# Up projection of a ConvFFN: block sums finished in PSUM under the convolution, four raw weight tiles, the next pair's weights prepared between the products, row sums partly on PE

## The chip, the cores and the metric

The kernel runs on one core of one Trainium2 chip. The metric is device time in microseconds (us) of one execution of the whole program. Engines are named as in the profile: PE is TensorE (matmul), DVE is VectorE, ACT is ScalarE, POOL is GpSimd, SP is SyncE, which here only issues DMAs.

## What is computed

One layer of an encoder trunk over 1024 tokens of width 1024: a hybrid mixer, a memory cross-attention and a gated MLP with a convolution of width three. The change touches the last of these alone:

```
gu = rms_norm(x, ffn_norm) @ w_up
gu = depthwise_conv(gu, ffn_conv_w, ffn_conv_b, FFN_CONV // 2, FFN_CONV // 2)
g, u = gu[..., :D_FF], gu[..., D_FF:]
x = x + (jax.nn.silu(g) * u) @ w_down
```

D_FF is 2816, so w_up has 5632 columns, and the up projection gives 22 blocks of 128 columns of g and the 22 blocks of u that belong to them. A block of g with its block of u is called a pair here.

## The kernel before

**Numbers.** Every matmul works in two parts: an operand is split into a rounded part and the remainder (ACT copies to the rounded type, DVE or POOL subtracts), and three matmuls per product (rounded by rounded, rounded by remainder, remainder by rounded) add up in PSUM. The normalised input h lies in SBUF transposed and split (`h3`), as 2 halves of 512 tokens.

**Up projection, plain pairs.** The first two pairs (`up_plain`, PLAIN is 2) are ordinary products: for g and u each, 24 matmuls of 128x512 for each of the two token halves, into a PSUM bank, which ACT copies (L1221) into an SBUF row.

**Up projection, fast pairs.** The other 20 pairs (`up_fast`) compute the 2x2 block product (rows of w_up in two halves, tokens in two halves) with seven block products instead of eight. `combos(k)` prepares, once for the stage, the needed sums T1 to T4 of the blocks of h: for each of four k, DVE (L1170 and neighbours) and POOL subtract the rounded parts and the remainders, and `put` splits the result again. For each pair POOL makes four sums S1 to S4 of the weight blocks, and `wop` splits seven weight operands. `prod` is one block product: 12 matmuls of 128x512. Products accumulate in three banks a_, b_ and c_: a_ takes w11 by B11 and then w12 by B21; b_ takes w2 by T2, then w3 by T3, then w22 by T4; c_ takes w1 by T1, then w4 by B22. Between them the block sums are read out: p1 (ACT, L1258) holds a_ after its first product, u2 (DVE, L1260) is b_ plus p1, p5 (ACT) is c_ after its first, u3 (DVE, L1267) is b_ after T3 plus p1. The results go into two SBUF rows `rows_` (a row for g, one for u): L1264 (ACT), L1268, L1270 and L1272 (DVE).

**Convolution and gate.** `gate` then works on the SBUF rows: for g and for u each, one ACT pass for the middle tap and the bias (L1201) and two DVE passes for the outer taps (L1202, L1203); then a tanh on ACT (L1207), two DVE passes (L1208, L1209) and a store of 512 KB to a scratch tensor `actd` in DRAM (L1210).

**Down projection.** For two halves of 512 tokens: 22 steps k, each loads a piece of actd (`ar`, L1297) and a piece of w_down (L1302), splits both, and runs 24 matmuls into eight banks. The residual tiles `xr` (L1292) are loaded at the start of each half.

**What sets the order.** The order in which each engine takes its instructions is fixed when the program is built: a scheduler with a simulated timeline interleaves the written code, so the products of one pair stand between those of the next. Each engine then runs its list strictly in that order, and waits on semaphores of the others. The tile pools track a tile as a whole (reuse_waits="tile"): an instruction that writes any part of a tile waits for the earlier readers of any part. The weight loads and the stores share SP's queue.

Of the kernel before, what the change touches and what calls it, by code (L numbers as in the profile page):

```python
# [83 lines left out]
def trunk_layer(ctx: ExitStack, tc: tile.TileContext, a: dict, out: bass.AP):  # L84
# [1076 lines left out]
    def combos(k):  # L1161

        d, e = tmpf("t3", "S1"), tmpf("e3", "S2")
        dve.tensor_sub(d, f(B22[0])[:, k, :], f(B12[0])[:, k, :])
# [5 lines left out]
        dve.tensor_sub(t1, f(B12[0])[:, k, :], f(B11[0])[:, k, :])  # L1170
# [24 lines left out]
    def gate(i):
        gu = []
        for s_ in range(2):
            jj = s_ * NF + i
# [2 lines left out]
            act.activation(g, r_[:, 1:S + 1], AF.Identity, bias=fcv[:, 3, jj:jj + 1], scale=fcv[:, 1, jj:jj + 1])  # L1201
            dve.scalar_tensor_tensor(g, r_[:, 0:S], fcv[:, 0, jj:jj + 1], g, ALU.mult, ALU.add)  # L1202
            dve.scalar_tensor_tensor(g, r_[:, 2:S + 2], fcv[:, 2, jj:jj + 1], g, ALU.mult, ALU.add)  # L1203
# [8 lines left out]
    def up_plain(i):  # L1212
        for s_ in range(2):
            with tc.issue_after(last_rs[-6 + s_ if i == 0 else -1].ins):
                wh, wl = wunit(up_load(i, s_))
            for c in (1, 0):
                ps = bank()
                for k in range(KD):
                    mm3(ps, wh[:, k * P:(k + 1) * P], wl[:, k * P:(k + 1) * P],
                        h3[c][0][:, k, :], h3[c][1][:, k, :], k == 0, k == KD - 1)  # L1220
                act.activation(rows_[s_][:, 1 + c * 512:513 + c * 512], ps, AF.Copy)  # L1221
# [118 lines left out]
```

## Time and profile before

| what | us |
|---|---|
| median of 3 runs (1516.84 to 1522.0) | 1517.36 |
| the profiled execution's own time | 1518.07 |
| its span | 1516.3 |
| plain pairs, from about | 768 |
| first fast pair, from about | 819 |
| fast pairs from the second, from about | 854 |
| up projection's last matmul, at | 1251.39 |
| down projection's first matmul, at | 1270.63 |

All times within the run are from the start of the span of one profiled execution, which is 0.7 us above the median. A row of the windows view gives, for a stretch of time, each engine's busy time with its count of instructions, then the clock that PE was granted (1.00 is full speed), the busy share of the DMA engines, and GB/s. A row of the timeline gives start, duration, engine, line, operation and tiles, and in square brackets how long the engine had been idle and what released it. PE's records carry a modelled end, so the distance from one start to the next is the better measure of its pace. In the groups by tile a row ends its name with the count, then least, median and largest duration in ns, the first and last start, and the shape.

### The profile page before, as it was taken

Reading aid. Unit: us, or ns where it says so; the run is one execution under the profiler, and the core shown is the slowest. Engines: PE = TensorE matmul, PEld = TensorE weight load, DVE = VectorE, ACT = ScalarE, POOL = GpSimd, SP = SyncE. Lnnn points to the kernel's source line nnn. Section 1 sums busy time; section 2 is a strip of 40 time slices with the busy share of each in tenths; the row PEclk is TensorE's granted clock in tenths of the full one; section 3 lists DMA queues with packets and bytes.
Section 4 is the critical chain, followed back from the end, with each engine's and each line's share of the span. In section 5 each row is a group of like instructions: output and inputs, shape, how many; then the busy total and the mean of one; then the engine's idle time right before and its main releaser. Section 6 shows DMA issues by size and latency. Waiting matters only on the chain.

```text
span 1516.3 us, 18284 instructions
## 1 busy us (share of the span) xinstructions
PE 1372.4 (91%) x6756; PEld 1147.3 (76%) x6756; DVE 1038.4 (68%) x1346; ACT 715.7 (47%) x1194; POOL 731.1 (48%) x688
## 2 busy tenths in 40 slices
PE   6887789898999999999977999999999995999998
PEld 5766678787888888888865777777777774888887
DVE  5889886899998854676688667667666693334332
ACT  5265665688888831455324434434444451222220
POOL 7768685556687610111374887776667600000000
PEclk9989889999999999999998899999999997999999
DMA  5211010200000141102210222122222235446541
GB/s 179 66 33 34 25 43 29 97 1 2 1 1 1 49 160 42 56 2 70 98 42 14 89 77 84 56 83 84 79 61 84 72 134 175 146 144 203 184 144 63
DMA packets 88024, 113.95 MB, mean 75 GB/s; under 512 B 6634, under 2 KB 61183, under 8 KB 87935
## 3 DMA queue, kind: packets, MB, share of 16 engines
q1 hardware_dynamic: 87935, 112.78, 23.0%
q8 instruction: 53, 0.87, 0.2%
q14 instruction: 36, 0.29, 0.1%
HBM read 92.84 MB, written 19.92 MB: 74 GB/s over the span
## 4 chain that ended last, share of the span: by engine, by line
PE 42%; DVE 19%; POOL 9%; DMA 5%; ACT 5%; issue 5%; SPq 0%; DVEq 0%; POOLq 0%; ACTq 0%
PE bank L109 16%; PE psP L109 5%; DMA raw<-in_w_up 5%; PE psq L109 3%; PE psmo L109 3%; PE psS L109 3%; PE po L109 2%; POOL S L1248 2%; DVE wop L1227 2%; DVE st L753 2%; POOL S L1243 2%; POOL S L1244 2%; DVE gu L1202 2%; DVE pT L776 2%; PE psT L772 2%
## 5 line engine op out<-in xcount | busy, mean ns | idle before, releaser
L109 PE MATMUL bank<-whi,ah 128*128 128x512 f32 x352 | 138.4, 393 | 18.8 <-ACT ah L1300 18.8
L109 PE MATMUL bank<-wlo,ah 128*128 128x512 f32 x352 | 138.1, 392 | 0.0
L109 PE MATMUL bank<-whi,al 128*128 128x512 f32 x352 | 135.6, 389 | 0.0
L1301 DVE TENSOR_TENSOR al<-ar,ah 128x512 fp32r<-128x512 f32 x44 | 30.4, 693 | 147.1 <-ACT ah L1300 138.3
L1227 POOL TENSOR_TENSOR wop<-S,wop 128x512 fp32r<-128x512 f32 x80 | 127.0, 1613 | 7.7 <-ACT wop L1226 7.7
L1234 PE MATMUL bank<-h,wop 128*128 128x512 f32 x320 | 125.6, 393 | 5.2 <-ACT p L1258 3.7
L1235 PE MATMUL bank<-h,wop 128*128 128x512 f32 x320 | 125.0, 391 | 0.0
L1236 PE MATMUL bank<-h,wop 128*128 128x512 f32 x320 | 124.5, 390 | 0.0
L1234 PE MATMUL bank<-T,wop 128*128 128x512 f32 x240 | 96.8, 403 | 30.4 <-DVE row L1272 14.5
L1300 ACT ACTIVATE ah<-ar 128x512 fp32r<-128x512 f32 x44 | 27.8, 632 | 177.3 <-PE bank L109 161.8
L109 PE MATMUL psS<-kT,qT 96*128 96x512 f32 x384 | 103.9, 404 | 5.3 <-ACT pr L757 5.2
L759 POOL TENSOR_SCALAR pr<-pr,st 128x1024 f32<-128x1024 f32 x64 | 72.0, 1126 | 53.9 <-DVE st L758 32.1
L1236 PE MATMUL bank<-T,wop 128*128 128x512 f32 x240 | 95.4, 398 | 2.8 <-POOL wop L1227 2.8
L1227 DVE TENSOR_TENSOR wop<-raw,wop 128x512 fp32r<-128x512 f32 x40 | 44.6, 1117 | 74.3 <-ACT wop L1226 58.2
L1235 PE MATMUL bank<-T,wop 128*128 128x512 f32 x240 | 95.2, 397 | 0.0
L1202 DVE SCALAR_TENSOR_TENSOR gu<-row,fcw,gu 128x1024 f32<-128x1024 f32 x44 | 68.6, 1560 | 34.3 <-ACT gu L1201 34.3
L109 PEld LDWEIGHTS bank<-whi,ah 128*128 128x128 f32 x352 | 66.9, 190 | 33.1 <-ACT ah L1300 19.3
L1226 ACT ACTIVATE wop<-S 128x512 fp32r<-128x512 f32 x80 | 47.6, 621 | 91.1 <-POOL S L1244 91.0
L776 DVE TENSOR_TENSOR pT<-psT,pT 128x512 fp32r<-128x512 f32 x128 | 84.5, 679 | 6.2 <-ACT pT L775 6.1
L109 PE MATMUL psin<-hT,whi 128*128 128x512 f32 (+1 forms) x288 | 87.4, 386 | 1.1 <-ACT hT L200 1.0
L757 ACT ACTIVATE pr<-psS,st,rqk 128x1024 f32<-128x1024 f32 x64 | 77.2, 1206 | 18.5 <-DVE st L755 14.0
L753 DVE TENSOR_REDUCE st<-psS 128x1 f32<-128x1024 f32 x64 | 77.7, 1214 | 8.0 <-PE psS L109 8.0
(347 smaller groups left out, 3877.5 us busy)
## 6 DMA issues: line engine op xcount, KB each, us to landing
raw<-in_w_up SPq DMA_DIRECT2D x44, 512.0 KB
raw<-in_w_down SPq DMA_DIRECT2D x44, 512.0 KB
actd<-th SPq DMA_DIRECT2D x22, 512.0 KB
...
```

What stands on the lines that cost most here:

```text
L109: return pe.matmul(ps, lhsT=l, rhs=r, start=start, stop=stop)
L753: dve.tensor_reduce(st[:, 0:1], psS, AX.X, ALU.max, negate=True)
L757: act.activation(pr, psS, AF.Exp, bias=st[:, 1:2], scale=r, accum_out=st[:, 2:3])
L759: scaled[s] = pool.tensor_scalar(pr, pr, st[:, 3:4], 0.0, ALU.mult, ALU.add)
L776: dve.tensor_sub(pTs[s // 2][n][1][:, :, qi * P:(qi + 1) * P], pv, f(dh))
L1202: dve.scalar_tensor_tensor(g, r_[:, 0:S], fcv[:, 0, jj:jj + 1], g, ALU.mult, ALU.add)
L1226: act.activation(o[:, :512], src, AF.Copy)
L1227: (pool if eng == "pool" else dve).tensor_sub(o[:, 512:], src, f(o)[:, :512])
L1234: pe.matmul(ps, lhsT=wh, rhs=bh, start=first and k == 0, stop=False, skip_group_check=True)
L1235: pe.matmul(ps, lhsT=wh, rhs=bl, start=False, stop=False, skip_group_check=True)
L1236: pe.matmul(ps, lhsT=wl, rhs=bh, start=False, stop=k == HK - 1, skip_group_check=True)
L1301: dve.tensor_sub(al, ar, f(ah))
```

## The change

A PSUM tile is now two banks wide (128x1024), and there are four. Each fast pair has two of them: G holds a_ and c_, the two token halves of g; U holds b_ and d_, those of u. The block sums are finished in place: DVE writes d_ = c_ + u3 (L1289), c_ += u2 (L1294) and b_ += p1 (L1298) into PSUM; p5, the SBUF rows and their copies are gone. The convolution (`conv`) reads the PSUM tile: ACT at L1199, DVE at L1200 and L1201 over 1023 columns. `p1` is copied at L1280, u2 made at L1283, u3 at L1288. Raw weights have four tiles, two each for g and u, and are loaded two pairs ahead; `prep` gives the next pair's sums and splits (L1225 on ACT, L1226 on DVE or POOL) as a list of steps, of which `run` puts one or two between the products. In `combos` the first two differences are made by 8 matmuls with plus and minus the identity (`idr`), 32 in all, and the other sums on DVE alone. The operands of the first two steps of the down projection are prepared at the end of the last pair (`first_down`); ah, al and ar take over tiles of the up projection, two of each; the residual tiles are loaded late in a half (the scheduler places them).

```diff
-    pf = psF.enter_context(tc.tile_pool(name="pf", bufs=8, space=PSUM, reuse_waits="tile"))
+    pf = psF.enter_context(tc.tile_pool(name="pf", bufs=4, space=PSUM, reuse_waits="tile"))
...
-    tpl = fs.enter_context(tc.tile_pool(name="tpl", bufs=3, side="right", reuse_waits="tile"))
+    tps = ExitStack()
+    tpl = tps.enter_context(tc.tile_pool(name="tpl", bufs=3, side="right", reuse_waits="tile"))
...
-    def bank():
-        return pf.tile([P, 512], F32, tag="bank", name="bank")
+    def banks():
+        return pf.tile([P, S], F32, tag="bank", name="bank")
...
+        ps = banks()
+        for o, x, y in ((0, B12, B11), (512, B22, B12)):
+            dst = ps[:, o:o + 512]
+            mm(dst, idr[:, 0], x[0][:, k, :], True, False)
+            mm(dst, idr[:, 0], x[1][:, k, :], False, False)
+            mm(dst, idr[:, 1], y[0][:, k, :], False, False)
+            mm(dst, idr[:, 1], y[1][:, k, :], False, True)
+        t1 = tmpf("t1", ("p1", "u2", "u3", "th")[k])
         t1s.append(t1)
...
+        act.activation(t1, ps[:, :512], AF.Copy)
+        put(T3, k, ps[:, 512:])
+        t2 = tmpf("t2", "S1")
+        dve.tensor_sub(t2, f(B22[0])[:, k, :], t1)
         dve.tensor_add(t2, t2, f(B22[1])[:, k, :])
         put(T2, k, t2)
...
+        t4 = tmpf("t4", "S2")
+        dve.tensor_sub(t4, f(B21[0])[:, k, :], t2)
         dve.tensor_add(t4, t4, f(B21[1])[:, k, :])
         put(T4, k, t4)
...
+    idr = fp.tile([P, 2, P], F32R, name="idr")
+    act.activation(idr[:, 0], ident, AF.Copy)
+    act.activation(idr[:, 1], ident, AF.Copy, scale=-1.0)
...
+        raw = (wp.tile([P, S], F32, tag="raw", bufs=2, name="rw") if s_ == 0 else
+               fp.tile([P, S], F32, tag="rw", bufs=2, name="rw"))
+        c0 = s_ * DFF + i * P
+        nc.sync.dma_start(raw.rearrange("p (k c) -> p k c", k=KD),
+                          a["w_up"][0, :, c0:c0 + P].rearrange("(k p) c -> p k c", p=P))
+        return raw
+
+    def conv(i, s_, ps):
+        jj = s_ * NF + i
+        g = fp.tile([P, S], F32, tag=("g", "u")[s_], name="gu")
+        act.activation(g, ps, AF.Identity, bias=fcv[:, 3, jj:jj + 1], scale=fcv[:, 1, jj:jj + 1])
+        dve.scalar_tensor_tensor(g[:, 1:], ps[:, :S - 1], fcv[:, 0, jj:jj + 1], g[:, 1:], ALU.mult, ALU.add)
+        dve.scalar_tensor_tensor(g[:, :S - 1], ps[:, 1:], fcv[:, 2, jj:jj + 1], g[:, :S - 1], ALU.mult, ALU.add)
+        return g
...
+    raws = {}
...
+    def prep(i):
+
+        if i >= NF:
+            return [], {}
+        rg, ru = raws.pop(i)
+        A11, A12, A21, A22 = rg[:, :512], rg[:, 512:], ru[:, :512], ru[:, 512:]
+        w, S_ = {}, {}
+
+        def split(name, src, eng):
+            def go():
+                v = src() if callable(src) else src
+                o = w[name] = wp.tile([P, 1024], F32R, tag="w", name="wop")
+                act.activation(o[:, :512], v, AF.Copy)
+                eng.tensor_sub(o[:, 512:], v, f(o)[:, :512])
+            return go
+
+        def summed(j, op, x, y):
+            def go():
+                S_[j] = tmpf(f"S{j}")
+                op(S_[j], x() if callable(x) else x, y() if callable(y) else y)
+            return go
+
+        steps = [split("11", A11, dve),
+                 summed(1, pool.tensor_add, A21, A22), summed(2, pool.tensor_sub, lambda: S_[1], A11),
+                 split("2", lambda: S_[2], dve), split("1", lambda: S_[1], pool),
+                 summed(3, pool.tensor_sub, A11, A21), split("3", lambda: S_[3], pool),
+                 split("12", A12, dve),
+                 summed(4, pool.tensor_sub, A12, lambda: S_[2]), split("4", lambda: S_[4], pool),
+                 split("22", A22, dve)]
+        return steps, w
...
+    def load_pair(i):
+        if i < NF:
+            raws[i] = (up_load(i, 0), up_load(i, 1))
...
+    def up_plain(i, nxt):
+        raw = raws.pop(i)
+        gu = []
+        for s_ in range(2):
+            wh, wl = wsplit(raw[s_])
+            ps = banks()
+            for c in (1, 0):
+                for k in range(KD):
+                    mm3(ps[:, c * 512:(c + 1) * 512], wh[:, k * P:(k + 1) * P], wl[:, k * P:(k + 1) * P],
+                        h3[c][0][:, k, :], h3[c][1][:, k, :], k == 0, k == KD - 1)
+            gu.append(conv(i, s_, ps))
+            for k in range((2 * i + s_) * HK // (2 * PLAIN), (2 * i + s_ + 1) * HK // (2 * PLAIN)):
+                combos(k)
+        gate(i, *gu)
...
+    def up_fast(i, w, nxt):
+        G, U = banks(), banks()
+        a_, c_, b_, d_ = G[:, :512], G[:, 512:], U[:, :512], U[:, 512:]
+        p1, u2, u3 = tmpf("p1"), tmpf("u2"), tmpf("u3")
+        prod(a_, w["11"], B11, True)
         act.activation(p1, a_, AF.Copy)
-        prod(b_, w2, T2, True)
+        run(nxt, 1)
+        prod(b_, w["2"], T2, True)
         dve.tensor_add(u2, b_, p1)
-        prod(c_, w1, T1, True)
-        act.activation(p5, c_, AF.Copy)
-        prod(a_, w12, B21, False)
-        act.activation(rG[:, lo], a_, AF.Copy)
-        prod(b_, w3, T3, False)
-        u3 = tmpf("u3")
+        run(nxt, 2)
+        prod(c_, w["1"], T1, True)
+        run(nxt, 2)
+        prod(b_, w["3"], T3, False)
         dve.tensor_add(u3, b_, p1)
-        dve.tensor_add(rU[:, hi], u3, p5)
-        prod(c_, w4, B22, False)
-        dve.tensor_add(rG[:, hi], c_, u2)
-        prod(b_, w22, T4, False)
-        dve.tensor_add(rU[:, lo], b_, p1)
-        gate(i)
-
+        dve.tensor_add(d_, c_, u3)
+        run(nxt, 2)
+        prod(a_, w["12"], B21, False)
+        run(nxt, 1)
+        prod(c_, w["4"], B22, False)
+        dve.tensor_add(c_, c_, u2)
+        g = conv(i, 0, G)
+        run(nxt, 2)
+        prod(b_, w["22"], T4, False)
+        dve.tensor_add(b_, b_, p1)
+        u = conv(i, 1, U)
+        run(nxt, len(nxt))
+        if i == NF - 1:
+            first_down.extend([down_in(0, 0), down_in(0, 1)])
+        gate(i, g, u)
+
+    def down_in(s_, k):
+        o = k % 2
+        ar = tmpf("ar", ("S1", "S2")[o])
+        nc.sync.dma_start(ar, actd[k, :, s_ * 512:(s_ + 1) * 512])
+        ah, al = tmpf("ah", ("S3", "S4")[o], F32R), tmpf("al", ("u2", "u3")[o], F32R)
+        act.activation(ah, ar, AF.Copy)
+        dve.tensor_sub(al, ar, f(ah))
+        wh, wl = wunit(lambda raw: nc.sync.dma_start(raw, a["w_down"][0, k * P:(k + 1) * P, :]), eng="ad")
+        return ah, al, wh, wl
...
+    with tc.issue_after(last_rs[-6].ins):
+        load_pair(0)
+    load_pair(1)
     for i in range(PLAIN):
-        up_plain(i)
-        for k in range(i * HK // PLAIN, (i + 1) * HK // PLAIN):
-            combos(k)
+        up_plain(i, None)
+        load_pair(i + 2)
...
+    nxt, w = prep(PLAIN)
+    run(nxt, 4)
...
+    run(nxt, len(nxt))
     for i in range(PLAIN, NF):
-        up_fast(i)
-    fs.close()
+        load_pair(i + 2)
+        nxt, w2 = prep(i + 1)
+        up_fast(i, w, nxt)
+        w = w2
+    tps.close()
 
...
-    dq = dn.enter_context(tc.tile_pool(name="dq", bufs=3, reuse_waits="tile"))
+    dq = dn.enter_context(tc.tile_pool(name="dq", bufs=3, side="right", reuse_waits="tile"))
...
     for s_ in range(2):
+        pss = [banks() for _ in range(4)]
+        ops = [down_in(s_, 0), down_in(s_, 1)] if s_ else first_down
+        for ts in ((0, 1), (2, 3)):
+            for k in range(2):
+                for t in ts:
+                    down_mm(pss[t], t, k, ops[k])
         xr_ = []
-        for t in range(4):
-            xt = dq.tile([P, D], F32, tag="xr", bufs=5, name="xr2")
-            nc.sync.dma_start(xt, x2d[s_ * 4 + t])
-            xr_.append(xt)
...
+        for k in range(2, NF):
+            ops = down_in(s_, k)
...
+            if k >= NF - 5 and len(xr_) < 4:
+                xt = dq.tile([P, D], F32, tag="xr", bufs=6, name="xr2")
+                nc.sync.dma_start(xt, x2d[s_ * 4 + len(xr_)])
+                xr_.append(xt)
```

**A fast pair in the middle.** On PE, of the change: G and U of pair n are bank_8426 and bank_8427, of pair n+1 bank_8567 and bank_8568, of n+2 bank_8708. One row stands for the 12 matmuls of a product (the first one; for w1 by T1 also the third); T1 is h310, B11 is h300.

```order
L1248 MATMUL bank_8427<-T3_7329,wop_8357 128x512 [waits DVE_49]
...
L1248 MATMUL bank_8568<-T2_7328,wop_8476 128x512 [waits DVE_49]
...
L1248 MATMUL bank_8426<-h300_6939,wop_8372 128x512 [waits DVE_49]
...
L1248 MATMUL bank_8426<-h310_7164,wop_8394 128x512
...
L1248 MATMUL bank_8427<-T4_7330,wop_8414 128x512
...
L1248 MATMUL bank_8567<-h310_7164,wop_8479 128x512 [waits Activation_49]
...
L1250 MATMUL bank_8567<-h310_7164,wop_8479 128x512 [waits Pool_49]
...
L1248 MATMUL bank_8708<-h300_6939,wop_8585 128x512 [waits DVE_49,PE_49]
```

And before: pair n has bank_8304 (a_), bank_8305 (b_) and bank_8306 (c_), pair n+1 bank_8449 to bank_8451, pair n+2 bank_8594.

```order
L1234 MATMUL bank_8306<-h310_7164,wop_8298 128x512 [waits Activation_49]
...
L1234 MATMUL bank_8450<-T2_7328,wop_8429 128x512
...
L1234 MATMUL bank_8451<-h310_7164,wop_8432 128x512
L1234 MATMUL bank_8304<-h300_6939,wop_8290 128x512 [waits Activation_49]
...
L1234 MATMUL bank_8305<-T3_7329,wop_8294 128x512 [waits DVE_49]
...
L1234 MATMUL bank_8594<-h300_6939,wop_8569 128x512
...
L1234 MATMUL bank_8305<-T4_7330,wop_8301 128x512 [waits DVE_49]
...
L1234 MATMUL bank_8451<-h310_7164,wop_8443 128x512 [waits Activation_49]
```

Before, the product w1 by T1 of pair n+1 (bank_8451) had a bank of its own and stood ahead of pair n's w12, w3 and w22 products; now it follows pair n's last product (bank_8427 by T4) and writes the same tile bank_8567 that p1 reads, with a wait on ACT.

On ACT, of the change, the same place: gu_8529 and gu_8551 are the convolutions of g and u of pair n, p1_8569 belongs to pair n+1, th_8558 is pair n's tanh.

```order
L1199 ACTIVATE gu_8529<-bank_8426,fcw_309 128x1024 [waits DVE_49]
L1225 ACTIVATE wop_8696<-rw_8424 128x512 [waits DMAHW0_49,PE_49]
L1199 ACTIVATE gu_8551<-bank_8427,fcw_309 128x1024 [waits DVE_49,Activation_49]
L1280 ACTIVATE p1_8569<-bank_8567 128x512 [waits Activation_49]
L1206 ACTIVATE th_8558<-gu_8529 128x1024 [waits DMAHW4_49,DVE_49,Activation_49]
```

On DVE, of the change, the same place:

```order
L1294 TENSOR_TENSOR bank_8426<-bank_8426,u2_8429 128x512 [waits PE_49]
L1200 SCALAR_TENSOR_TENSOR gu_8529<-bank_8426,fcw_309,gu_8529 128x1023 [waits Activation_49]
L1298 TENSOR_TENSOR bank_8427<-bank_8427,p1_8428 128x512 [waits PE_49]
L1226 TENSOR_TENSOR wop_8696<-rw_8424,wop_8696 128x512 [waits DMAHW0_49,Activation_49]
L1201 SCALAR_TENSOR_TENSOR gu_8529<-bank_8426,fcw_309,gu_8529 128x1023 [waits DVE_49]
L1200 SCALAR_TENSOR_TENSOR gu_8551<-bank_8427,fcw_309,gu_8551 128x1023 [waits Activation_49]
L1283 TENSOR_TENSOR u2_8570<-bank_8568,p1_8569 128x512 [waits Activation_49]
```

p1 of pair n+1 stands on ACT behind both convolution passes of pair n, the second of which waits on DVE (L1298); L1298 stands on DVE behind the first convolution pass of DVE (L1200), which waits for ACT's L1199.

**The start of the plain pairs.** On DVE, before: L917 makes the remainders of the last two groups of h, L1170 the first differences of `combos`.

```order
L917 TENSOR_TENSOR h311_7165<-psn_7288,h310_7164 128x4x128 [waits Activation_49]
L1170 TENSOR_TENSOR t1_7473<-h310_7164,h300_6939 128x512 [waits DVE_49,PE_49]
L1170 TENSOR_TENSOR t1_7495<-h310_7164,h300_6939 128x512
L1170 TENSOR_TENSOR t1_7646<-h310_7164,h300_6939 128x512
L1170 TENSOR_TENSOR t1_7668<-h310_7164,h300_6939 128x512
L917 TENSOR_TENSOR h311_7165<-psn_7295,h310_7164 128x4x128 [waits Activation_49]
```

And in the change:

```order
L917 TENSOR_TENSOR h311_7165<-psn_7288,h310_7164 128x4x128 [waits Activation_49]
L917 TENSOR_TENSOR h311_7165<-psn_7295,h310_7164 128x4x128 [waits Activation_49]
L1226 TENSOR_TENSOR wop_7680<-rw_7507,wop_7680 128x512 [waits DMAHW1_49,Activation_49]
L1200 SCALAR_TENSOR_TENSOR gu_7395<-bank_7346,fcw_309,gu_7395 128x1023 [waits Activation_49]
```

The four differences stood between the two L917 and are gone from DVE.

**From up to down.** On SP, before, behind the last pair's store (th_10586):

```order
L1302 DMA raw_10870<-in_w_down 128x1024
L1210 DMA actd_7306<-th_10586 128x1024
L1292 DMA xr2_10596<-x2d_7305 128x1024
...
L1292 DMA xr2_10602<-x2d_7305 128x1024
L1297 DMA ar_10612<-actd_7306 128x512
L1297 DMA ar_10648<-actd_7306 128x512
```

And in the change, first the loads of the first two steps, then what stands behind the store of the pair before the last (th_10387):

```order
L1312 DMA raw_10501<-in_w_down 128x1024
...
L1308 DMA ar_10507<-actd_7306 128x512
L1308 DMA ar_10495<-actd_7306 128x512
...
L1209 DMA actd_7306<-th_10250 128x1024
```

```order
L1209 DMA actd_7306<-th_10387 128x1024
L1312 DMA raw_10694<-in_w_down 128x1024
L1308 DMA ar_10616<-actd_7306 128x512
L1312 DMA raw_10730<-in_w_down 128x1024
L1308 DMA ar_10580<-actd_7306 128x512
L1358 DMA xr2_11156<-x2d_7305 128x1024
...
L1358 DMA xr2_12014<-x2d_7305 128x1024
L1312 DMA raw_10766<-in_w_down 128x1024
```

The first two loads of ar moved ahead of three stores; six residual loads now stand ahead of a w_down load of a later step (raw_10766), and before, four of them stood ahead of the first ar.

More of the change, by code (lines that the diff above doesn't have):

```diff
@@ L1150, in trunk_layer, with tmpf @@
     T2, T3, T4 = tnew("T2"), tnew("T3"), tnew("T4")
-    def tmpf(name, tag=None):
-        return fp.tile([P, 512], F32, tag=tag or name, name=name)
+    def tmpf(name, tag=None, dt=F32):
+        return fp.tile([P, 512], dt, tag=tag or name, name=name)
     def put(dst, k, v):
@@ L1210, in gate @@
         nc.sync.dma_start(actd[i], th)
[L1212 to L1221, printed above, removed]
-        gate(i)
-    def wop(src, eng="pool"):
-        o = wp.tile([P, 1024], F32R, tag="w", name="wop")
-        act.activation(o[:, :512], src, AF.Copy)
-        (pool if eng == "pool" else dve).tensor_sub(o[:, 512:], src, f(o)[:, :512])
-        return o
+    raws = {}
[25 more added lines that the diff above has]
+        return steps, w
     def prod(ps, w, b, first):
@@ L1236, in prod, with run @@
             pe.matmul(ps, lhsT=wl, rhs=bh, start=False, stop=k == HK - 1, skip_group_check=True)
-    def up_fast(i):
-        rg, ru = wload(up_load(i, 0)), wload(up_load(i, 1))
-        A11, A12, A21, A22 = rg[:, :512], rg[:, 512:], ru[:, :512], ru[:, 512:]
-        S1, S2, S3, S4 = [tmpf(f"S{j}") for j in range(1, 5)]
-        w11 = wop(A11)
-        pool.tensor_add(S1, A21, A22)
-        pool.tensor_sub(S2, S1, A11)
-        w2 = wop(S2)
-        w1 = wop(S1)
-        w12 = wop(A12, "dve")
-        pool.tensor_sub(S3, A11, A21)
-        w3 = wop(S3)
-        pool.tensor_sub(S4, A12, S2)
-        w4 = wop(S4)
-        w22 = wop(A22, "dve")
-        rG, rU = rows_
-        lo, hi = slice(1, 513), slice(513, 1025)
-        a_, b_, c_ = bank(), bank(), bank()
-        p1, u2, p5 = tmpf("p1"), tmpf("u2"), tmpf("p5")
-        prod(a_, w11, B11, True)
+    def run(steps, n):
+        for _ in range(min(n, len(steps))):
+            steps.pop(0)()
@@ L1287, in trunk_layer @@
-    dq = dn.enter_context(tc.tile_pool(name="dq", bufs=3, reuse_waits="tile"))
-    for s_ in range(2):
-        xr_ = []
-        for t in range(4):
-            xt = dq.tile([P, D], F32, tag="xr", bufs=5, name="xr2")
-            nc.sync.dma_start(xt, x2d[s_ * 4 + t])
-            xr_.append(xt)
-        pss = [[bank() for _ in range(2)] for _ in range(4)]
-        for k in range(NF):
-            ar = dq.tile([P, 512], F32, tag="ar", name="ar")
-            nc.sync.dma_start(ar, actd[k, :, s_ * 512:(s_ + 1) * 512])
-            ah = dq.tile([P, 512], F32R, tag="ah", name="ah")
-            al = dq.tile([P, 512], F32R, tag="al", name="al")
-            act.activation(ah, ar, AF.Copy)
-            dve.tensor_sub(al, ar, f(ah))
-            wh, wl = wunit(lambda raw: nc.sync.dma_start(raw, a["w_down"][0, k * P:(k + 1) * P, :]), eng="ad")
-            for t in range(4):
-                for half in range(2):
-                    mm3(pss[t][half], ah[:, t * P:(t + 1) * P], al[:, t * P:(t + 1) * P],
-                        wh[:, half * 512:(half + 1) * 512], wl[:, half * 512:(half + 1) * 512], k == 0, k == NF - 1)
+        load_pair(i + 2)
```

45 lines of the change are left out of this document (10 added, 35 removed).

## The prediction

> **What bounds the kernel now.** First the windows, cut at the stages of the feed-forward part (columns: span; busy time of PE, weight loads, DVE, ACT, POOL; granted clock; DMA share; GB/s).
>
> ```profile
> span 1516.3 us, 18284 instructions
> 768.00:819.00 51.00, 46.47 (x195) 37.56 (x194) 46.28 (x40) 15.29 (x24) 33.56 (x24) 0.95 0.10 32
> 819.00:854.00 35.00, 23.33 (x86) 18.16 (x85) 22.32 (x22) 16.98 (x27) 26.82 (x17) 0.76 0.14 45
> 854.00:1229.00 375.00, 351.04 (x1515) 283.47 (x1515) 258.33 (x231) 159.51 (x235) 258.62 (x162) 1.00 0.26 79
> 1229.00:1252.00 23.00, 20.02 (x84) 15.25 (x83) 21.79 (x24) 10.75 (x12) 0.00 (x0) 1.00 0.40 138
> 1252.00:1271.00 19.00, 0.37 (x1) 0.38 (x2) 7.71 (x8) 2.82 (x3) 0.00 (x0) 0.57 0.64 220
> 1271.00:1516.30 245.30, 241.45 (x1056) 199.35 (x1055) 86.47 (x98) 63.51 (x81) 0.00 (x0) 0.99 0.44 146
> ```
>
> PE carries every stage but the fifth, 19 us in which it does almost nothing between up and down. How fast PE can go stands in the timeline: the rows are the first matmul of one product and of the next.
>
> ```profile
> 1060.76 0.39 PE L1234 MATMUL bank<-T,wop 128*128 128x512 f32 x1
> 1063.48 0.39 PE L1234 MATMUL bank<-h,wop 128*128 128x512 f32 x1
> ```
>
> Twelve matmuls take 2.72 us, 0.2265 each, so the seven products of a pair take 19.04 us. The third row (854 to 1229) holds 18 pairs: 375.0 against 18 x 19.04 = 342.7, so 32.3 us are lost there; the last pair loses 23.0 - 19.04 = 4.0, the first fast pair 35.0 - 19.04 = 16.0. Up's fast pairs can thus give at most 52 us, the transition 19, the plain start some 6 (below). PE's waits between 854 and 1252 name the loss (total, times, longest):
>
> ```profile
> PE bank L1234 <- DVE row L1272: 14.5, 10, 3.0
> ```
>
> PE waits for a bank until DVE has read it into the row. That reader goes, and one of its cases shows what a longer stall costs. Here are the last matmul before it and the first after, then three windows of 3.41 us; then another, shorter stall with its windows.
>
> ```profile
> 1021.92 0.39 PE L1236 MATMUL bank<-h,wop 128*128 128x512 f32 x1
> 1025.26 0.47 PE L1234 MATMUL bank<-T,wop 128*128 128x512 f32 x1 [2.96 <-DVE row L1272]
> 1019.28:1022.69 3.41, 3.03 (x14) 2.17 (x12) 0.00 (x0) 1.30 (x3) 3.33 (x4) 1.00 0.00 0
> 1022.69:1026.10 3.41, 0.84 (x4) 0.74 (x5) 1.96 (x2) 1.84 (x3) 3.41 (x4) 1.00 0.05 10
> 1026.10:1029.52 3.42, 3.42 (x10) 2.68 (x9) 3.09 (x3) 1.30 (x3) 2.47 (x2) 0.50 0.48 143
> 1088.93 0.47 PE L1234 MATMUL bank<-T,wop 128*128 128x512 f32 x1 [2.03 <-DVE row L1272]
> 1084.13:1087.55 3.42, 2.77 (x13) 1.96 (x11) 0.75 (x1) 2.19 (x4) 3.34 (x3) 1.00 0.00 0
> 1087.55:1090.96 3.41, 2.03 (x9) 1.71 (x10) 2.09 (x3) 2.15 (x3) 3.04 (x3) 1.00 0.40 117
> 1090.96:1094.37 3.41, 3.41 (x17) 2.81 (x16) 3.41 (x4) 0.74 (x2) 1.70 (x1) 1.00 0.13 39
> ```
>
> The clock changes on a grid of 3.413 us. In the first case PE was busy 0.84 of 3.41 us (idle 75%), and the window behind it was granted 0.50: its 3.42 us of work cost 1.7 us extra. In the second the idle time fell into two windows, the worse one idle 1.38 of 3.41 (40%), and the clock held.
>
> **The wait that the change adds.** On PE the product w1 by T1 of pair n+1 now follows pair n's last product directly, and it writes the PSUM tile that p1 of pair n+1 (L1280, ACT) reads, so it waits for p1. On ACT p1 stands behind the u convolution of pair n (L1199), which waits for b_ += p1 (L1298) on DVE, which stands behind L1200 of the g convolution, which waits for ACT's L1199, and that for c_ += u2 (L1294), which waits for pair n's w4 product. So from the end of w4 by B22 seven passes run in single file between two engines, beside one product of PE, w22 by T4. Their durations, from the nearest operations of before (a group's three figures are least, median, largest in ns):
>
> ```profile
> L757 ACT ACTIVATE pr<-psS,st,rqk 128x1024 f32<-128x1024 f32 x64 | 77.2, 1206 | 18.5 <-DVE st L755 14.0
> L1270 DVE TENSOR_TENSOR row<-bank,u x20: 677/680/693, 851.8 to 1245.2; 128x512 f32<-128x512 f32 x20
> L1258 ACT ACTIVATE p<-bank x20: 572/578/582, 835.4 to 1241.5; 128x512 f32<-128x512 f32 x20
> L1202 DVE SCALAR_TENSOR_TENSOR gu<-row,fcw,gu x44: 1272/1471/2422, 794.1 to 1255.5; 128x1024 f32<-128x1024 f32 x44
> 1244.77 0.39 PE L1236 MATMUL bank<-h,wop 128*128 128x512 f32 x1
> 1245.26 0.60 ACT L1264 ACTIVATE row<-bank 128x512 f32<-128x512 f32 x1 [2.21 <-PE bank L1236]
> 1251.46 1.28 DVE L1203 SCALAR_TENSOR_TENSOR gu<-row,fcw,gu 128x1024 f32<-128x1024 f32 x1
> 1252.78 1.06 ACT L1207 ACTIVATE th<-gu 128x1024 f32<-128x1024 f32 x1 [2.67 <-DVE gu L1203]
> 1253.74 1.23 ACT L1201 ACTIVATE gu<-row,fcw 128x1024 f32<-128x1024 f32 x1
> 1269.94 0.63 ACT L1300 ACTIVATE ah<-ar 128x512 fp32r<-128x512 f32 x1 [14.97 <-DMA ar<-actd]
> 1270.63 0.80 PE L109 MATMUL bank<-whi,ah 128*128 128x512 f32 x1 [18.85 <-ACT ah L1300]
> ```
>
> From the start of w4's last matmul: 0.49 until its reader starts (1244.77 to 1245.26); L1294 0.68 (as L1270); 0.04 from DVE to ACT (1252.74 to 1252.78); L1199 on g 1.21 (as L757, the same shape from PSUM); 0.04 back; L1200 1.28; L1298 0.60 (0.68, less 0.08 by which queued passes overlap, as on ACT at 1253.74); 0.04; L1199 on u 1.21; p1 0.48 (0.58 less 0.10); 0.06 to PE (1270.57 to 1270.63). Sum 6.13. PE alone would start w1 by T1 after 13 x 0.2265 = 2.94. **The stall is 3.2 us**, at 19 places (pairs 2 to 20 of the fast ones), in place of 36.3 us lost before (32.3 + 4.0). Lower end 2.9 (the hand-overs, 0.28 in all, at nothing), upper 3.4 (L1200 at 1471, the median of L1202). I take 3.1, a little under the sum, since a hand-over is read to some 0.05 from these rows; and L1200 at its least, since it reads PSUM like L1270, whose times hardly vary (677 to 693).
>
> Then the clock. Of a stall of 3.1, some 2.9 us are idle (as 2.96 of the 3.34 between the starts above). By the two cases the limit for one window lies between 1.4 and 2.6 us idle; I take 2.0. 2.9 us put on a grid of 3.41 leave 2.0 in one window for (1.4 + 0.9) / 3.41 = 67% of places. But the place is not random: a pair with both losses lasts 19.04 + 3.1 + 1.7 = 23.8 us, 6.98 windows, so the next stall falls on the same place of the grid; a pair that escapes lasts 22.1, 6.49 windows, and the next stall is moved by half a window, to where it is caught. So 17 of 19 are caught: 17 x 1.7 = 28.9. [...]
>
> **The sum, against the profiled 1518.07.**
>
> 1. Added matmuls with the identity: 32 x 0.2265 = **+7.2**. They stand among the plain pairs, where PE is the limit. Ends: 0 (in a stall that is there anyway) and 7.2.
>
> 2. Plain start.
>
> ```profile
> 769.09 7.45 DVE L1170 TENSOR_TENSOR t<-h,h 128x512 f32<-128x512 f32 x4
> 772.27 0.39 PE L109 MATMUL bank<-h,whi 128*128 128x512 f32 x1
> 777.19 0.80 PE L109 MATMUL bank<-h,whi 128*128 128x512 f32 x1 [4.53 <-DVE h L917]
> 776.93:780.34 3.41, 3.15 (x7) 2.51 (x8) 3.09 (x4) 0.28 (x1) 2.49 (x2) 0.50 0.17 48
> ```
>
> PE waits 4.9 - 0.2 = 4.7 us for L917, behind the four L1170; with the half-clock window behind it (1.7) that is **-6.4** once they are gone from DVE. Late next is the split of the weights on POOL, which was ready here. Ends: -6.4 and 0.
>
> 3. First fast pair, 16.0 us lost before, most of it at one place:
>
> ```profile
> 832.77 0.80 PE L1234 MATMUL bank<-T,wop 128*128 128x512 f32 x1 [10.50 <-ACT wop L1226]
> ```
>
> The weight sums S1 and S2 use the SBUF of t2 and t4 of `combos`, so they wait for the last `put`; that stays so. POOL's part of the sums goes to DVE, which in the same stretch now has the plain pairs' convolution. I take two thirds of the loss as staying, **-5.9**; ends -16 and 0.
>
> 4. Pairs 2 to 20: 19 x 3.1 + 28.9 + 2.0 (the last pair has no product of a later pair to cover d_ = c_ + u3 before w12: 3 x 0.68 in a row) = 89.8, less 36.3: **+53.5**. Ends: +21 without the clock and at 2.9 (55.1 + 2.0 - 36.3), +62 at 3.4 with all 19 caught (64.6 + 32.3 + 2.0 - 36.3).
>
> 5. Up to down. Before, the chain was the last pair's store, four residual loads, then ar:
>
> ```profile
> 1251.39 0.39 PE L1236 MATMUL bank<-T,wop 128*128 128x512 f32 x1
> 1259.83 3.73 SPq L1292 DMA_DIRECT2D xr<-x2d  x4
> 1263.66 1.58 SPq L1297 DMA_DIRECT2D ar<-actd  x3
> ```
>
> The first two steps need only stores of pairs 0 and 1 and are loaded early, so 19.0 us go, and about 2.4 of half clock behind them (the last window row: 245.3 at 0.99). In their place: six residual loads (3 MB; at the fifth row's 220 GB/s 14 us) stand ahead of a later w_down load and of ar of step 4, while steps 0 to 3 give 4 x 24 x 0.2265 = 21.7 us of cover. Cover gone, it costs some 6. I take 3.4 back: **-18**; ends -21.4 and -14.
>
> 6. Cost nothing: the four raw tiles (loads ran at 0.26 of the DMA engines and no wait for them is among PE's), the copies into rows that are gone (their engines have room: DVE 258 of 375), and the down stage otherwise, PE-bound at 241 of 245.
>
> 7.2 - 6.4 - 5.9 + 53.5 - 18 = +30.4, so 1548.5; less the 0.7 by which the profiled run is over the median: **1548**.
>
> **The rivals.** [...] *The wait is covered*, the way to a faster kernel: if p1 came in time (the records would show w1 by T1 starting within 0.3 of the product before), pairs lose 0.5 each to hand-overs, 19 x 0.5 + 2 instead of 89.8: 78 less, so 1470. Its point of decision is the place of p1 on ACT: ahead of the u convolution, 1470; behind it, 1548. Against it: p1's place in ACT's list is fixed, and the sum of seven passes is twice the cover. *Longer stalls or more half clock*: a window behind the half-clock one also granted 0.50, as after the first fast pair, where the whole stretch had 0.76; if half the stalls did this, 9 x 1.7 = 15 more, or with 3.4 us a stall 6 more: 1554 to 1565.
>
> **How the numbers follow.** Forecast with its own range 1538 to 1556: 0.63. Clock holds: 0.16. Covered: 0.10. Longer: 0.11. The range 1510 to 1565 takes in the forecast, the clock-holds case with its unknown terms, and most of the longer one; it leaves out the covered one and tails. A measurement of this kernel tells about 0.5%, 7.6 us, from no change. Faster: 0.11 (covered, and a little of clock-holds); within: 0.13; slower: 0.76.
>
> **What would show it.** PE's waits: some 19 of the first w1 by T1 matmul on ACT's p1, of 2.9 to 3.1 us each, 55 to 60 us in all; windows of 0.50 clock in nearly every pair, and pairs of 23.8 us. If the windows stay at 1.00, pairs last 22.1. If there is no such wait, the forecast is wrong at its root. No gap of more than 4 us at the start of the plain pairs and none of 19 before down; one product of delay at most in down's steps 3 to 5.

## The result and the profile after

| | us |
|---|---|
| before, median of 4 runs (1516.84 to 1522.0) | 1517.87 |
| change, median of 4 runs (1559.31 to 1565.8) | 1562.04 |
| ratio, with its 95% interval | 1.0287 (1.0259 to 1.0316) |
| span of the change's profiled run (1559.31 us) | 1557.5 |

The change is slower by 2.9%, 44 us by the medians and 41.2 by the two profiled spans. First PE's waits in the change, between 750 and 1320 us (total, times, longest; the one at L912 lies just ahead of the plain pairs):

```profile
PE bank L1248 <- ACT p L1280: 54.3, 18, 3.0
PE bank L1248 <- ACT wop L1225: 9.5, 1, 9.5
PE bank L1248 <- DVE bank L1289: 3.9, 2, 2.9
PE psn L912 <- DVE nxs L903: 3.7, 1, 3.7
PE bank L109 <- ACT gu L1199: 2.5, 1, 2.5
```

The wait for DVE's row is gone, and a wait for p1 stands 18 times in its place, 54.3 us in all. One of them in the timeline: PE, then ACT, then DVE.

```profile
934.21 0.39 PE L1250 MATMUL bank<-T,wop 128*128 128x512 f32 x1
937.62 0.50 PE L1248 MATMUL bank<-h,wop 128*128 128x512 f32 x1 [3.03 <-ACT p L1280]
932.65 1.21 ACT L1199 ACTIVATE gu<-bank,fcw 128x1024 f32<-128x1024 f32 x1
935.88 1.21 ACT L1199 ACTIVATE gu<-bank,fcw 128x1024 f32<-128x1024 f32 x1 [0.61 <-DVE bank L1298]
936.98 0.59 ACT L1280 ACTIVATE p<-bank 128x512 f32<-128x512 f32 x1
931.92 0.70 DVE L1294 TENSOR_TENSOR bank<-bank,u 128x512 f32<-128x512 f32 x1 [0.33 <-PE bank L1250]
933.89 1.28 DVE L1200 SCALAR_TENSOR_TENSOR gu<-bank,fcw,gu 128x1023 f32<-128x1023 f32 x1 [1.28 <-ACT gu L1199]
935.10 0.69 DVE L1298 TENSOR_TENSOR bank<-bank,p 128x512 f32<-128x512 f32 x1
```

Read by start times the rows make one chain: DVE 931.92, ACT 932.65, DVE 933.89 and 935.10, ACT 935.88 and 936.98, PE 937.62. Each step of it has to wait for the one before, so the two engines take turns. PE's last matmul began at 934.21, so at 0.2265 from start to start the next could have begun at 934.44: the stall is 3.18 us. The windows of the clock's grid around it, and then the stages of the feed-forward part, as in the windows of before:

```profile
934.87:938.28 3.41, 0.66 (x3) 0.57 (x4) 3.41 (x5) 2.71 (x4) 0.47 (x1) 1.00 0.19 56
938.28:941.69 3.41, 3.41 (x10) 2.64 (x9) 3.40 (x4) 0.43 (x1) 0.00 (x0) 0.50 0.34 101
941.69:945.11 3.42, 3.42 (x17) 2.81 (x16) 1.90 (x2) 0.68 (x2) 0.00 (x0) 1.00 0.38 152
...
771.00:823.50 52.50, 52.49 (x224) 43.01 (x225) 28.65 (x36) 15.73 (x24) 11.80 (x7) 0.97 0.15 45
823.50:862.50 39.00, 26.66 (x109) 21.11 (x108) 26.77 (x27) 16.04 (x27) 32.84 (x21) 0.87 0.25 75
862.50:1293.50 431.00, 376.68 (x1513) 303.01 (x1512) 255.24 (x271) 151.36 (x197) 152.43 (x119) 0.93 0.21 67
1293.50:1314.00 20.50, 16.92 (x67) 13.24 (x66) 14.37 (x16) 6.91 (x7) 0.00 (x0) 0.92 0.35 117
1314.00:1557.50 243.50, 238.77 (x1053) 197.05 (x1051) 93.92 (x104) 65.16 (x82) 0.00 (x0) 1.00 0.48 161
```

PE is busy 0.66 of the first 3.41 us, and the window behind it is granted 0.50. The same happens 18 times between 862.5 and 1293.5: 431.0 us for 18 pairs' 126 products (342.5 us), 88.5 lost, of which 18 x 3.18 = 57.2 are stall and the rest, 31.3, is 1.7 us of half clock each. The first and the last of the 18, each with the window ahead of it:

```profile
863.19:866.60 3.41, 0.92 (x4) 0.79 (x5) 3.41 (x5) 1.89 (x3) 3.41 (x3) 1.00 0.02 7
866.60:870.01 3.41, 3.41 (x10) 2.61 (x9) 3.41 (x5) 1.06 (x1) 1.31 (x2) 0.50 0.54 152
...
1269.38:1272.79 3.41, 0.53 (x3) 0.10 (x1) 3.41 (x4) 2.86 (x4) 0.00 (x0) 1.00 0.01 2
1272.79:1276.20 3.41, 3.33 (x8) 2.65 (x9) 3.41 (x5) 1.09 (x2) 0.00 (x0) 0.50 0.00 0
```

From 866.60 to 1272.79 a window at 0.50 comes every 23.89 us, 7 windows of 3.413. The last row of the stages, above, begins where the up projection ends; the empty stage of 19 us is gone.

### The profile page after: what moved, and what is told of

It is laid out like the page before. It is cut to its first block, busy times and chain, and to the rows that moved or that the text cites. A ratio compares the mean times of both kernels' runs of the same rounds, so it can differ in the third digit from the quotient of the medians.

```text
span 1557.5 us, 18253 instructions
## 1 busy us (share of the span) xinstructions
PE 1404.7 (90%) x6788; PEld 1173.4 (75%) x6788; DVE 1013.3 (65%) x1378; ACT 702.9 (45%) x1152; POOL 600.5 (39%) x628
## 4 chain that ended last, share of the span: by engine, by line
PE 62%; DVE 13%; ACT 4%; POOL 4%; issue 3%; DMA 0%; DVEq 0%; ACTq 0%; POOLq 0%
PE bank L109 18%; PE bank L1248 8%; PE bank L1249 7%; PE bank L1250 7%; PE psP L109 5%; PE psmo L109 3%; PE psS L109 3%; PE po L109 3%; PE psq L109 2%; DVE st L753 2%; ACT gu L1199 2%; PE psT L772 2%; DVE gu L1201 1%; DVE pT L776 1%; DVE gu L1200 1%
## 5 line engine op out<-in xcount | busy, mean ns | idle before, releaser
L1248 PE MATMUL bank<-h,wop 128*128 128x512 f32 x320 | 140.2, 438 | 58.2 <-ACT p L1280 54.3
L1226 POOL TENSOR_TENSOR wop<-S,wop 128x512 fp32r<-128x512 f32 x60 | 81.5, 1360 | 251.8 <-ACT wop L1225 249.9
L1249 PE MATMUL bank<-h,wop 128*128 128x512 f32 x320 | 136.8, 428 | 0.0
L1250 PE MATMUL bank<-h,wop 128*128 128x512 f32 x320 | 135.4, 423 | 0.0
L1248 PEld LDWEIGHTS bank<-h,wop 128*128 128x128 f32 x320 | 67.4, 211 | 81.6 <-ACT p L1280 62.2
L1226 DVE TENSOR_TENSOR wop<-rw,wop 128x512 fp32r<-128x512 f32 x60 | 66.9, 1120 | 88.0 <-ACT wop L1225 87.9
L1225 ACT ACTIVATE wop<-S 128x512 fp32r<-128x512 f32 x80 | 49.8, 631 | 164.1 <-PE bank L1250 145.7
L1248 PE MATMUL bank<-T,wop 128*128 128x512 f32 x240 | 94.0, 392 | 9.5 <-ACT wop L1225 9.5
L1249 PE MATMUL bank<-T,wop 128*128 128x512 f32 x240 | 93.8, 391 | 0.0
L1250 PE MATMUL bank<-T,wop 128*128 128x512 f32 x240 | 93.7, 390 | 0.0
L1200 DVE SCALAR_TENSOR_TENSOR gu<-bank,fcw,gu 128x1023 f32<-128x1023 f32 x44 | 56.3, 1278 | 45.7 <-ACT gu L1199 45.7
L757 ACT ACTIVATE pr<-psS,st,rqk 128x1024 f32<-128x1024 f32 x64 | 77.2, 1207 | 17.9 <-DVE st L755 13.3
L1225 ACT ACTIVATE wop<-rw 128x512 fp32r<-128x512 f32 x60 | 37.6, 630 | 104.6 <-PE bank L1250 104.6
```

The lines of the kernel that those rows point to most:

```text
L757: act.activation(pr, psS, AF.Exp, bias=st[:, 1:2], scale=r, accum_out=st[:, 2:3])
L1200: dve.scalar_tensor_tensor(g[:, 1:], ps[:, :S - 1], fcv[:, 0, jj:jj + 1], g[:, 1:], ALU.mult, ALU.add)
L1225: act.activation(o[:, :512], v, AF.Copy)
L1226: eng.tensor_sub(o[:, 512:], v, f(o)[:, :512])
L1248: pe.matmul(ps, lhsT=wh, rhs=bh, start=first and k == 0, stop=False, skip_group_check=True)
L1249: pe.matmul(ps, lhsT=wh, rhs=bl, start=False, stop=False, skip_group_check=True)
```

## The experiments

All are the change with one thing altered, unless it is said otherwise.

**Filling the stall.** The nine matmuls into d_ belong to no result.

```diff
         prod(b_, w["2"], T2, True)
+        if last22:
+            with tc.issue_after(last22[-1].ins):
+                for _ in range(9):
+                    pe.matmul(d_, lhsT=idr[:, 0], rhs=B12[0][:, 0, :], start=True, stop=True, skip_group_check=True)
         dve.tensor_add(u2, b_, p1)
...
-        prod(b_, w["22"], T4, False)
+        last22.append(prod(b_, w["22"], T4, False))
```

> Nine matmuls that nothing uses (2.04 us of PE, into d_, which is overwritten later) stand directly behind w22 by T4 of the pair before, so that PE idles some 0.9 us instead of 2.9 before w1 by T1; the wait for p1 itself is untouched. Theory (a window that is idle by more than about 2 us costs the next one half its clock): no 0.50 windows in the fast pairs, the starts of w1 by T1 still 3.2 us late, pairs of 22.2 us instead of 23.9, so 18 x 1.7 = 31 us less than the change: about 1531. Rival (the half clock comes from something other than PE's idle time, such as the load on all engines): windows of 0.50 stay, 1555 to 1566.

Measured: 1530.3 (1528.3 to 1537.9, six runs). A stall in the timeline, the window in which it lies, and the windows row from 863 to 1249:

```profile
932.57 1.07 PE L1289 MATMUL bank<-h,idr 128*128 128x512 f32 x4
934.62 0.50 PE L1248 MATMUL bank<-h,wop 128*128 128x512 f32 x1 [0.98 <-ACT p L1283]
...
932.40:935.81 3.41, 2.43 (x11) 1.71 (x10) 3.41 (x5) 2.76 (x3) 0.00 (x0) 1.00 0.31 93
...
863.00:1249.00 386.00, 368.39 (x1602) 299.02 (x1601) 243.34 (x261) 148.09 (x194) 154.17 (x121) 1.00 0.22 71
```

The clock stays at 1.00 in the fast pairs, a pair takes 22.37 us in place of 23.95, and the product still waits for p1. More work on PE made the kernel 31.7 us faster than the change. Here only PE's idle time was altered (0.98 us of this window, 2.75 of the one at 934.87 in the change), so the half clock is shown to come from it.

**p1 ahead of the u convolution, one buffer and two.** The next pair's tiles, its w11 product and p1 are written behind the g convolution (`head`); with two buffers p1 has the tags p1 and p1b in turn.

```diff
+    def head(i, w):
+        if i >= NF:
+            return None
+        G, U, p1 = banks(), banks(), tmpf("p1", ("p1", "p1b")[i % 2])
+        prod(G[:, :512], w["11"], B11, True)
+        act.activation(p1, G[:, :512], AF.Copy)
+        return G, U, p1
...
         g = conv(i, 0, G)
+        hd = head(i + 1, w2)
```

> The next pair's w11 product and its copy p1 are written ahead of the u convolution, so that on ACT p1 stands ahead of the second L1199; p1 keeps its one buffer, so it waits for b_ += p1 of the pair before. Theory (the chain c_, L1199, L1200, b_, L1199, p1 in single file sets the stall): the stall loses one ACT pass of 1.2 us, 3.2 to 2.0, PE idle 1.8 of a window of 3.41 at most, so no half clock: 18 x (1.2 + 1.7) = 52 less, about 1510. Rival (PE waits for DVE in some other place as well, for instance u2 or d_, once p1 is early): the gain is given back and the time is 1540 or more.

> As the run with p1 early, and p1 has two buffers, used in turn, so that it waits for its own product alone. Theory (the wait for p1 is the whole loss of pairs 2 to 20): w1 by T1 starts behind the product before it, pairs of 19.1 to 19.6 us, 18 x (3.2 + 1.7) = 88 less than the change, less up to 9 for other hand-overs: 1474 to 1483. Rival (DVE, whose list of a pair is some 15.6 us plus waits, or the PSUM tiles become the bound): pairs of 20.5 as before the change, 1498 or more.

Measured: one buffer 1523.3 (1520.9 to 1524.6, eight runs), two buffers 1476.4 (1475.4 to 1477.4, two runs). With one buffer, a stall, and two stalls' windows with the one behind each:

```profile
949.79 0.39 PE L1250 MATMUL bank<-T,wop 128*128 128x512 f32 x1
952.10 0.50 PE L1248 MATMUL bank<-h,wop 128*128 128x512 f32 x1 [1.92 <-ACT p L1280]
...
1125.22:1128.63 3.41, 1.56 (x7) 1.30 (x8) 3.41 (x6) 2.72 (x4) 0.65 (x1) 1.00 0.10 29
1128.63:1132.05 3.42, 3.42 (x17) 2.83 (x16) 3.42 (x4) 1.26 (x2) 0.00 (x0) 1.00 0.45 131
...
992.10:995.51 3.41, 1.48 (x7) 0.92 (x6) 3.41 (x4) 2.15 (x3) 1.28 (x1) 1.00 0.23 69
995.51:998.92 3.41, 3.41 (x10) 2.64 (x9) 3.41 (x5) 1.24 (x2) 0.00 (x0) 0.50 0.52 154
```

The stall is 2.31 - 0.23 = 2.1 us, as expected (2.0). But the expectation that the clock would hold was wrong: eight of the stalls still cost a half-clock window, which is the 13 us between 1510 and 1523. In these two windows 1.85 us idle did not lower the clock, and 1.93 did. The limit can't be set that closely, though: a window of the run with t2 and t4 moved, below, lowered it at 1.79.

With two buffers, the steady stretch, and PE's waits in it:

```profile
870.00:1200.00 330.00, 326.21 (x1422) 265.31 (x1421) 231.89 (x256) 140.56 (x188) 161.46 (x116) 1.00 0.25 80
...
PE bank L1248 <- DVE gu L1201: 3.2, 8, 0.4
PE bank L1248 <- DVE bank L1295: 0.6, 1, 0.6
```

PE is busy 326 of 330 us, and no wait for p1 is left; a pair takes 19.5 us on average. The change loses 85.6 us to p1's place and its buffer. The rival (DVE or the tiles as the bound, 1498 or more) is out: DVE is busy 232 of 330.

**The first fast pair's wait.** t2 and t4 of `combos` take other tiles.

```diff
-        t2 = tmpf("t2", "S1")
+        t2 = tmpf("t2", "S3")
...
-        t4 = tmpf("t4", "S2")
+        t4 = tmpf("t4", "S4")
```

> t2 and t4 of combos use the SBUF of S3 and S4 instead of S1 and S2. Theory (the 9.5 us wait of the first fast pair is POOL's first sum waiting for the put of T2, whose SBUF it takes over): the sums S1 and S2 are made during the plain pairs, the gap at 826 shrinks from 9.9 to about 3, with its half-clock windows: 6 to 10 us less than the change, 1552 to 1556. Rival (the last puts on DVE are late by themselves): the gap stays over 8, and the time within 3 us of the change.

Measured: 1559.7 (1556.8 and 1562.5). In the change POOL's first sum waited for T2, then PE for the split of a sum. The first row is POOL's first sum in the change; then three of PE's waits with the edit, and two windows of the first fast pair with it:

```profile
829.34 4.52 POOL L1232 TENSOR_TENSOR S<-rw 128x512 f32<-128x512 f32 x1 [46.37 <-DVE T L1158]
...
PE bank L1248 <- ACT p L1280: 55.1, 18, 3.8
PE psn L912 <- DVE nxs L903: 3.7, 1, 3.7
PE bank L1248 <- ACT wop L1225: 2.7, 1, 2.7
...
845.87:849.28 3.41, 1.62 (x8) 1.02 (x7) 3.41 (x4) 2.19 (x4) 3.41 (x3) 1.00 0.61 177
849.29:852.70 3.41, 3.41 (x10) 2.67 (x9) 2.75 (x4) 1.23 (x3) 3.41 (x3) 0.50 0.28 83
```

The mechanism was right: the wait of 9.5 us is down to 2.7. The gain was not. Shorter waits came in its place (1.8 us for L1226 on DVE, in the first window, 0.6 for POOL), PE worked in two more windows at half clock (one is the last row), 1.7 us each, and these took up half: the fast stage (first to last matmul) went from 490.1 only to 486.9 us. Besides, this run began its plain pairs 6 us later than the change's (see below), so the total says nothing.

**The identity matmuls undone**: `combos` as before the change.

```diff
-        ps = banks()
-        for o, x, y in ((0, B12, B11), (512, B22, B12)):
...
+        d, e = tmpf("t3", "S1"), tmpf("e3", "S2")
+        dve.tensor_sub(d, f(B22[0])[:, k, :], f(B12[0])[:, k, :])
+        pool.tensor_sub(e, f(B22[1])[:, k, :], f(B12[1])[:, k, :])
...
+        pool.tensor_sub(t2, f(B22[0])[:, k, :], t1)
```

> The first two differences of combos are made on DVE and POOL again, as before the change, and the 32 matmuls with the identity are gone. Theory (they cost 32 x 0.2265 = 7.2 us where PE is the limit): the plain stage, 52.7 us from its first matmul to the first fast one in the change, takes 45.5 if DVE's remainder of h is not late again, or 50 to 51 with the stall of 4.7 us of before. Rival (the matmuls fill stalls that are there anyway): 52 or more. The whole time moves with it, and with the first fast pair, by which the single run is the weaker witness.

Measured: 1563.9 (1562.6 and 1565.2), no clear difference from the change. The plain stage, and PE's wait in the first fast pair:

```profile
771.00:816.80 45.80, 45.70 (x194) 37.14 (x194) 39.88 (x35) 10.62 (x16) 33.92 (x20) 0.96 0.16 50
...
PE bank L1248 <- ACT wop L1225: 17.9, 1, 17.9
```

45.7 us in place of 52.7: the 32 matmuls cost their full 7 us. PE's wait for L917 did not come back, though three of the differences (3.81 us; 7.45 for four before) stand ahead of it on DVE again. But PE's wait for the first split in the fast stage rose from 9.5 to 17.9 us, the fast stage from 490.1 to 500.1. What the new `combos` costs in one stage it brings back in the next, where the sums are awaited. How much of that the matmuls bring is not shown: the edit also gives POOL its four sums back, and POOL is busy 33.92 us in this stage, 11.80 in the change.

**ar, ah and al late.** No first_down, and tiles of the pool `dq`.

```diff
-        ar = tmpf("ar", ("S1", "S2")[o])
+        ar = dq.tile([P, 512], F32, tag="ar", name="ar")
...
-            first_down.extend([down_in(0, 0), down_in(0, 1)])
```

> ar, ah and al of the down projection are again tiles of their own, in SBUF that the up projection's T tiles hold until their last product; they still stand ahead of the residual loads in SP's queue. Theory (before, ar waited for the last pair's store and four residual loads, 8 us after up's end to their issue and some 6 behind them): with these out of the way what stays is one load of 256 KB and ACT's copy, so the gap between up and down is 4 to 7 us instead of 0.2 in the change (19.2 before), and the time 4 to 9 more than the change, clock included. Rival (the early start alone made the gain of 19): the gap is 15 or more.

Measured: 1567.1 (1566.3 and 1568.0), 5 above the change. The kernel before, beside this run, took 1521.2, some 3 more than beside the change, so the profile is the better witness.

```profile
1315.12 0.39 PE L1250 MATMUL bank<-T,wop 128*128 128x512 f32 x1
1318.82 0.79 PE L109 MATMUL bank<-whi,ah 128*128 128x512 f32 x1 [3.31 <-ACT ah L1309]
```

A gap of 3.7 us in place of 0.2, and 2.0 us more in the down stage behind it. So of the 21 us gained around this place the early tiles bring 5 or 6. The rest goes with ar's place in SP's queue, ahead of the last store and of the residual loads; those two were not taken apart.

**Two raw weight tiles**, in the kernel with two buffers of p1.

```diff
-        raw = (wp.tile([P, S], F32, tag="raw", bufs=2, name="rw") if s_ == 0 else
-               fp.tile([P, S], F32, tag="rw", bufs=2, name="rw"))
+        raw = wp.tile([P, S], F32, tag="raw", bufs=2, name="rw")
```

> The run with two buffers of p1, with two raw weight tiles instead of four, so that a pair's weights can be loaded only when the pair before has read its own. Theory (the loads have room): a load starts behind the split of w22 near the end of a pair and lands 3 to 6 us later, the first split needs it some 5 us into the next pair, a pair ahead of its product: 0 to 1 us a pair, 1476 to 1495. Rival (four tiles carry the gain): S1 and S2 on POOL come late, pairs of 21 us or more, 1510 or more.

Measured: 1493.9 (1492.9 and 1494.9), 17.5 above the one with four.

```profile
890.00:1220.00 330.00, 326.46 (x1432) 267.64 (x1430) 247.36 (x257) 139.30 (x188) 169.81 (x116) 1.00 0.26 83
...
880.21 0.79 PE L1247 MATMUL bank<-T,wop 128*128 128x512 f32 x1 [4.64 <-DVE u L1288]
```

In the steady pairs nothing changes (326 of 330 us again), so the loads have room there. What is lost lies at the start: 7.8 us in the first fast pairs (one wait of 4.6 in them), and 9 us ahead of the plain pairs, whose cause this one profile does not settle.

**All together.** Two buffers of p1, t2 and t4 in S3 and S4, and the combos a step earlier.

```diff
-            for k in range((2 * i + s_) * HK // (2 * PLAIN), (2 * i + s_ + 1) * HK // (2 * PLAIN)):
+            for k in ((0,), (1, 2), (3,), ())[2 * i + s_]:
                 combos(k)
```

> Two buffers of p1, next pair's w11 product written early, t2 and t4 in the SBUF of S3 and S4, and the four combos one step earlier (none in the last plain half). Theory (the first fast pair's wait is POOL's sums behind the put of T2, and that put behind the last plain half's work): the gap of 9.9 us and most of the 13.7 us of half clock in the fast stage go, which are 9.7 + 6.8 = 16 at most: 1460 to 1468, 0.962 to 0.967 of before. Rival (DVE's convolution in the last plain half is the limit there): 1470 or more.

Measured: 1471.2 (1467.4 to 1476.4, six runs), 0.9685 of before (0.9659 to 0.9711): faster than both kernels, and above the 1460 to 1468 that were expected, in the range of the rival.

```profile
822.40:860.00 37.60, 34.18 (x145) 26.38 (x144) 28.93 (x27) 16.85 (x26) 30.62 (x21) 1.00 0.33 98
860.00:1200.00 340.00, 336.86 (x1469) 274.39 (x1469) 235.33 (x259) 143.21 (x191) 160.81 (x115) 1.00 0.26 83
1200.00:1222.00 22.00, 19.27 (x71) 15.09 (x70) 15.59 (x18) 7.62 (x7) 0.00 (x0) 0.84 0.33 108
...
PE bank L1248 <- DVE bank L1295: 2.0, 1, 2.0
PE bank L1250 <- DVE wop L1226: 0.8, 1, 0.8
PE bank L1248 <- DVE gu L1201: 0.6, 1, 0.6
```

The gap of 9.9 us and the half clock at the first fast pair are gone (0.87 in the change, 1.00 here), as the theory said, but less was gained than it allowed. PE's waits that are left in the first stretch (the last three rows) are all for DVE, so the rival has a share. The fast stage is 399.3 us against 406.7 with two buffers alone, a gain of 7.4 where 16 was the most, and against 380.5 of pure products. What is left is spread over the three stretches (by the count of matmuls at 0.2265: 4.8, 7.3 and 5.9 us), most densely in the last pair, where no later product covers the wait for d_.

**The change once more.**

> The change itself, a second time, to see how much of the 2.3 us by which its plain pairs begin later than before (770.9 to 768.6) belongs to the run. If it is the order of the earlier, unchanged part: 770.5 to 771.5 again. If it is the run: anything from 766 to 777, as in the other kernels' profiles (768.6 to 781.3). The fast stage 490 in both cases.

Measured: 1562.2. The plain pairs began at 774.0 (770.9 in the first profile, 768.6 before the change), the fast stage took 490.0. The same program moves by 3 us in a part that the change does not touch, so 2 or 3 us there are the run's and not the change's.

## Why the prediction came out

It said slower, at 1548 with a range of 1510 to 1565, and 1562 was measured. The mechanism is the one that was named, in its order and its place; the sizes of the fast stage were low. The time lies outside the forecast's own 1538 to 1556 and among those given for longer stalls or more half clock (1554 to 1565), yet that rival did not come: a stall took 3.18 us, not 3.4, and one window behind it ran at 0.50, not two. The 11 us by which the profiled run is over the sum are smaller misses, most of them in the fast stage.

- **The wait.** Seven passes in single file, 3.1 us: measured 3.18. The chain above is the sum's list of terms, each within 0.1 us. Shown by taking it away: with p1 early and in two buffers the 18 waits are gone, and 85.6 us with them. It came 18 times and not 19: in the last pair, two down matmuls and the wait for L1199 (2.5 us) stand where the nineteenth would be.
- **The clock.** "17 of 19 caught, 1.7 each": 18 of 18, 1.7 each. The windows at 0.50 are 23.89 us apart and pairs of 23.95 are 0.06 longer, so from one stall to the next the place on the grid hardly moved, and every window ahead of them had 2.49 us idle (the one at 863.19) or more. A window with PE busy 0.66 of 3.41 us (934.87) and, with p1 early, one with 1.48 (992.10) were followed by 0.50. The case of a clock that holds, with its chance of 0.16, stood for the sum without these 28.9 us, 1519; it is out.
- **Pairs 2 to 20, +53.5.** From 862.5 to 1293.5 they lost 88.5 us against 18 x 3.1 + 28.9 = 84.7, some 4 low: 1.4 by the 3.1 that was taken under the sum's own 3.2, the rest by the clock. The fast stage as a whole lost 490.1 - 380.5 = 109.6, which leaves 6.8 for the last pair against 3.1 + 2.0. So this term was some 5.5 low.
- **The first fast pair, -5.9: the term of the fast stage that was off most for its size.** It was argued that two thirds of the loss would stay. In the stretch 823.5 to 862.5 14.3 us are lost (39.0 less 109 matmuls at 0.2265) against 10.1 forecast. Some 11.4 of them are the wait for the first split (9.65) with its half clock (1.7): POOL's first sum waited for the put of T2 and then ran 4.52 us where its neighbours take 1.3 to 1.7, 3.4 us of that time beside a busy DVE. The other 3.0 are a second wait, for d_ = c_ + u3, which the sum had in the last pair alone; here u3 (L1288) stands on DVE behind three splits:

```profile
848.10 4.73 DVE L1226 TENSOR_TENSOR wop<-rw,wop 128x512 fp32r<-128x512 f32 x3 [0.34 <-ACT wop L1225]
852.76 0.68 DVE L1288 TENSOR_TENSOR u<-bank,p 128x512 f32<-128x512 f32 x1
854.22 0.50 PE L1248 MATMUL bank<-h,wop 128*128 128x512 f32 x1 [2.85 <-DVE bank L1289]
```

- **Identity matmuls and plain start, +7.2 and -6.4.** The stage took 52.7 us in place of 50.8: +1.9 against +0.8. Undone, the 7 us show up by themselves, and so does what the new `combos` gives back at the first fast pair, which the sum did not see.
- **Up to down, -18.** 19.2 to 0.2 us, and the down stage 245.7 to 243.7: -21. The 3.4 us that six residual loads were to take back did not come.
- **Rest.** Some 2 us ahead of the plain pairs, no more than the same program moves there from run to run.

By the profiled spans the parts are 2.3 + 1.9 + 58.1 - 21.0 = 41.3: ahead of the plain pairs, plain stage, fast stage (490.1 against 432.0), up to down. The forecast's +30.4 was right in sign and cause; its fast stage was +47.6 and should have been +58.
